# Layer B's weights of keys, values and output projection: high and low parts made by rounding and adding transfers in place of Vector's subtraction

## The chip, the cores and the metric

The kernel runs on one core of a Trainium2 chip. The metric is the device time of one execution in microseconds (us). The engines that matter are TensorE (PE, matmuls; PEld is its weight load), VectorE (DVE), ScalarE (ACT), GpSimd (POOL), and SyncE (SP), which here only issues transfers. Each engine works through its own instructions strictly in order. A transfer (DMA) is issued by SP, ACT or POOL and is then carried out by 16 DMA engines that all issuers share; whoever needs the data waits on a semaphore.

## The reference, cut to what matters

Two layers with 512 tokens and width 1024. The second layer, B, computes (leaving out what the change does not touch):

```
s_in = rmsnorm(h, ln_shared)
kvf  = s_in @ w_shared_kv            # keys 768 | values 768 | forget gate 12
q    = rmsnorm(h, ln_mix_pre) @ w_in_b
main = forgetting_attention(q, k, v, log_f)      # 12 heads of 64, blocks of 128 queries
mixed = concat([main, memory_attention(q_mem, mem_n, w_mem_kv)])
h = h + rmsnorm(mixed @ w_out, ln_mix_post)      # then the feed-forward part
```

All of it is float32. The matrices that the change touches are the key part and the value part of `w_shared_kv` and the `w_out` of layer B.

## The kernel before, in words

**Products of two parts.** TensorE is fed with a rounded float32 format (`F32R`). To keep accuracy each operand is held as a high part (the value rounded) and a low part (the value less its high part), and a product is three matmuls, high by high, low by high and high by low (`mm3`; L174 to L176 are its lines). So every weight has to be made into two parts before TensorE can use it. Before, that goes as follows: SP loads 128 x 1024 floats (512 KB) into a buffer `raw` (four of these exist, and every weight of the kernel goes through them); for each half of 512 columns ACT copies into `hi`, which rounds (L222), and Vector subtracts, `lo = raw - hi` (L223). `hi` and `lo` have eight half-size buffers each. As soon as the two splits are done, `raw` is free for the next load.

```
def split(src, hi, lo, eng=None):
    A.copy(hi, src)
    (eng or V).tensor_sub(lo, src, hi)
```

**Layer B.** Its work around the change runs in this order. The query weights go through four blocks of a `boundary` with the feed-forward part before, and four more (`ps` in the trace). Then the products of keys and values: three value blocks of two loads each, six key blocks of one load each. These are cut into pieces (a value piece is 12 matmuls, a key piece 6), and a list `fill` sets each block's loading three pieces before its first piece. Six pieces run at once; the others are strewn between the steps of the attention heads, four memory heads and twelve forgetting heads, to give TensorE something to do while a head's softmax (DVE and ACT) runs. During the heads' last part the pieces of the output projection's first half (`out_part`, blocks of columns dh 0 and dh 1 with two loads each, matmuls called `y<-whi,mixedhi` in the trace) take the place of the keys and values. What remains of the projection (`mix_tail`, four loads) runs after the heads, two of its four loads into other buffers ("aside").

**A head.** Per block of 128 queries: logits on TensorE (`lg`), the row maximum on DVE (L412), the exponential on ACT (L413), the normalisation on DVE (`p<-p,sm`, L422), transposes on TensorE (`tr`), their two parts by ACT and DVE (`pT`), and the product with the values (`o`, L497). ACT and DVE do these in line with the splitting of the weights.

**What sets the order.** The kernel is written against a framework that assigns each engine its sequence of instructions when the program is built, by its own estimate of when operands will be there. The order is fixed after that, and each engine waits at an instruction until its semaphores are met. POOL does very little before the change: a few power functions for the norms (L237) and four copies of 128 KB between halves of the memory keys (`memk`, L364). SP issues the weight loads and, for each pair of heads, transfers that lay out query and key parts (L1194 to L1196).

Of the kernel before, what the change touches and what calls it, by code (L numbers as in the profile page):

```python
# [8 lines left out]
F32R = mybir.dt.float32r  # L9
BF16 = mybir.dt.bfloat16  # L10
AF = mybir.ActivationFunctionType
ALU = mybir.AluOpType
# [3 lines left out]
P = 128  # L16
T = 512
D = 1024
KT = 8
# [21 lines left out]
def hybrid(ctx: ExitStack, tc: tile.TileContext, i: dict, out: bass.AP):  # L41
# [5 lines left out]
    wp = ctx.enter_context(tc.tile_pool(name="weights", bufs=4))  # L47
# [4 lines left out]
    last_load, last_exp = [None], [None]  # L52

    def name(s):
        n_of[s] = n_of.get(s, 0) + 1
        return f"{s}_{n_of[s]}"

    def act(s, dt=F32R, shape=(P, T)):
        return ap.tile(list(shape), dt, tag="a", name=name(s))

    def plain(s, shape=(P, T), dt=F32):
        return yp.tile(list(shape), dt, tag="y", name=name(s))
# [10 lines left out]
    def ps(tag, shape=(P, T), s="ps"):  # L73
        return pp.tile(list(shape), F32, tag=tag, name=name(s), bufs=2 if tag == "tr" else 3)

    V, A, PE, G = nc.vector, nc.scalar, nc.tensor, nc.gpsimd
# [37 lines left out]
    def pair_of_parts(n=512, aside=False):  # L114
        if aside:
            return act("whi"), act("wlo")
        return (wp.tile([P, 512], F32R, tag="hi", name=name("whi"), bufs=8)[:, :n],
                wp.tile([P, 512], F32R, tag="lo", name=name("wlo"), bufs=8)[:, :n])
# [11 lines left out]
    def prepared(src, shape, eng=None):  # L130

        raw = wp.tile([P, 1024], F32, tag="raw", name=name("raw"), bufs=4)
        n = shape[0] * shape[1]
        dst = raw[:, :n].rearrange("p (a b) -> p a b", a=src.shape[1]) if len(src.shape) == 3 else raw[:, :n]
        last_load[0] = nc.sync.dma_start(dst, src)
        return weight_parts(raw, shape, eng)

    def weight_parts(raw, shape, eng=None):
        n = shape[0] * shape[1]
        parts = []  # L140
        for d in range(0, n, 512):
            pair = pair_of_parts(min(512, n - d))
            split(raw[:, d : min(d + 512, n)], *pair, eng)
            parts += cut(pair, shape[1])
        return parts

    def moving_pair(src, aside=False):

        raw = wp.tile([P, 1024], F32, tag="raw", name=name("raw"), bufs=4)
        last_load[0] = nc.sync.dma_start(raw.rearrange("p (m c) -> p m c", m=4), src)  # L150
        four = raw.rearrange("p (m k c) -> p m k c", m=4, k=2)
        parts = []
        for x in range(2):
            hi, lo = (t.rearrange("p (m c) -> p m c", m=4) for t in pair_of_parts(aside=aside))
            split(four[:, :, x, :], hi, lo)
            parts.append((hi, lo))
        return parts

    def out_weights(layer, kp, dh, aside=False):
        return moving_pair(i["w_out"][layer, 4 * dh : 4 * dh + 4, :, 256 * kp : 256 * kp + 256]  # L160
                           .rearrange("m p c -> p m c"), aside)

    def down_weights(layer, k, dh, aside=False):
        return moving_pair(i["w_down"][layer, 4 * dh : 4 * dh + 4, :, k : k + 2, :]
                           .rearrange("m p k c -> p m (k c)"), aside)
# [6 lines left out]
    def mm3(o, w, x, start, stop, more=False):  # L172

        PE.matmul(o, w[0], x[0], start=start, stop=False, skip_group_check=more)  # L174
        PE.matmul(o, w[0], x[1], start=False, stop=False, skip_group_check=more)  # L175
        PE.matmul(o, w[1], x[0], start=False, stop=stop, skip_group_check=more)  # L176
# [44 lines left out]
# [3 lines that stand above are left out]
# [525 lines left out]
    def out_part(layer, mixed):  # L749


        ys = [[None] * 2 for _ in range(TB)]

        def block(dh):
            w, o = [], []

            def load():
                for kp in range(2):
                    w.extend(out_weights(layer, kp, dh))

            def piece(tb, n):
                if n == 0:
                    o.append(ps("mm", s="y"))
                for k in range(2 * n, 2 * n + 2):
                    token_products(o[tb], mixed[ORDER[k]], w[k], tb, k == 0, k == 3)
                if n == 1:
                    ys[tb][dh] = plain("y")
                    A.copy(ys[tb][dh], o[tb])

            return load, [lambda tb=tb, n=n: piece(tb, n) for tb in range(TB) for n in range(2)]  # L770

        return ys, [block(dh) for dh in range(2)]

    def mix_tail(layer, mixed, ys):
        return tail_of([mixed[k] for k in ORDER[4:]], lambda kp, dh, aside: out_weights(layer, 2 + kp, dh, aside), ys)
# [263 lines left out]
    def layer_b(phase, fp):  # L1039
# [34 lines left out]
        def key_block(m):  # L1074

            w, o = [], []

            def load():
                w.extend(prepared(i["w_k"][m], (KT, P)))

            def piece(n):
                if n == 0:
                    o.append(ps("mm", s="k"))
                for k in range(2 * n, 2 * n + 2):
                    mm3(o[0], w[k], s_act[k], k == 0, k == KT - 1)
                if n == 3:
                    keys.append(act("k", F32))
                    V.tensor_mul(keys[m], o[0], rbc)

            return load, [lambda n=n: piece(n) for n in range(4)]  # L1090

        def value_block(j):

            w, o = [], []

            def load():
                for kh in range(2):
                    w.extend(prepared(i["w_v"][j, kh], (4, 256)))

            def piece(tk, kh):  # L1100
                if kh == 0:
                    o.append(ps("mm", (P, 256), s="v"))
                c = slice(tk * P, (tk + 1) * P)
                for k in range(4 * kh, 4 * kh + 4):
                    mm3(o[tk], (s_act[k][0][:, c], s_act[k][1][:, c]), w[k], k == 0, k == KT - 1)
                if kh:
                    if tk % 2 == 0:
                        vals[j, tk // 2] = plain("vf", (P, 2, 256))
                    V.tensor_scalar_mul(vals[j, tk // 2][:, tk % 2, :], o[tk], r4b[:, tk : tk + 1])

            return load, [lambda tk=tk, kh=kh: piece(tk, kh) for tk in range(TB) for kh in range(2)]
# [11 lines left out]
        for k in range(KT):  # L1123
            w = wfs[:, k, :, :].rearrange("p a b -> p (a b)")
# [74 lines left out]
        for n in range(HEADS):  # L1199
            pr, j = divmod(n, 2)  # L1200
# [114 lines left out]
```

## Time and profile before

| | us |
|---|---|
| median of 3 runs | 1136.09 |
| lowest, highest | 1135.89, 1137.71 |
| the profiled execution's own time | 1135.76 |
| its span, first to last instruction | 1134.0 |
| PE busy in the span | 1112.0 (98%) |
| DVE busy | 897.7 (79%) |
| ACT busy | 657.4 (58%) |
| POOL busy | 24.1 (2%) |
| layer B's heads, in the span | about 604 to 745 |

How to read it: a row of work says start, duration, engine, line, operation, and output<-inputs with their shapes; where idle time came before it, a bracket at the end names what ended that idle time. PE's matmuls overlap in the pipeline, so one that shows 0.39 us may follow the one ahead by 0.23 us. Buffer numbers are left out in the trace's names; in the lists of order below they are kept.

### The profile page before, as it was taken

Reading aid. Unit: us, or ns where it says so; the run is one execution under the profiler, and the core shown is the slowest. Engines: PE = TensorE matmul, PEld = TensorE weight load, DVE = VectorE, ACT = ScalarE, POOL = GpSimd, SP = SyncE. Lnnn points to the kernel's source line nnn. Section 1 sums busy time; section 2 is a strip of 40 time slices with the busy share of each in tenths; the row PEclk is TensorE's granted clock in tenths of the full one; section 3 lists DMA queues with packets and bytes.
Section 4 is the critical chain, followed back from the end, with each engine's and each line's share of the span. In section 5 each row is a group of like instructions: output and inputs, shape, how many; then the busy total and the mean of one; then the engine's idle time right before and its main releaser. Section 6 shows DMA issues by size and latency. Waiting matters only on the chain.

```text
span 1134.0 us, 19608 instructions
## 1 busy us (share of the span) xinstructions
PE 1112.0 (98%) x7437; PEld 1018.8 (90%) x7437; DVE 897.7 (79%) x1727; ACT 657.4 (58%) x1367; POOL 24.1 (2%) x42
## 2 busy tenths in 40 slices
PE   7999999999999999999999999999999999999997
PEld 6998889999899898997978998889999899899995
DVE  7979558898698588786957889958998588588775
ACT  6665458665266254476737667858765266255453
POOL 1000000000000000001000000000000000000000
PEclk9999999999999999999999999999999999999999
DMA  8412231325234233243232455521134224233222
GB/s 280 133 45 93 92 95 57 114 93 156 67 112 131 61 107 112 78 148 129 78 110 73 115 125 136 137 90 43 62 120 149 75 83 141 75 106 118 75 75 75
DMA packets 63814, 118.13 MB, mean 104 GB/s; under 512 B 5164, under 2 KB 39992, under 8 KB 63720
## 3 DMA queue, kind: packets, MB, share of 16 engines
q1 hardware_dynamic: 63384, 116.31, 33.2%
q8 instruction: 58, 0.95, 0.3%
q0 software_dynamic: 192, 0.52, 0.2%
q14 instruction: 36, 0.29, 0.1%
q10 hardware_dynamic: 144, 0.05, 0.0%
HBM read 104.71 MB, written 2.10 MB: 94 GB/s over the span
## 4 chain that ended last, share of the span: by engine, by line
PE 83%; DVE 8%; ACT 4%; DMA 2%; issue 2%; POOL 0%; SPq 0%; POOLq 0%; DVEq 0%; ACTq 0%
PE y L176 8%; PE y L175 8%; PE y L174 8%; PE a L175 5%; PE a L174 5%; PE a L176 5%; PE ps L174 4%; PE ps L175 4%; PE ps L176 4%; PE e L174 3%; PE e L176 3%; PE e L175 3%; PE x L176 3%; PE x L175 3%; PE x L174 3%
## 5 line engine op out<-in xcount | busy, mean ns | idle before, releaser
L222 ACT CAST whi<-raw 128x512 fp32r<-128x512 f32 x460 | 276.6, 620 | 267.4 <-PE y L176 111.2
L223 DVE TENSOR_TENSOR wlo<-raw,whi 128x512 fp32r<-128x512 f32 x460 | 306.4, 686 | 114.6 <-ACT whi L222 110.3
L174 PE MATMUL y<-whi,fhi 128*128 128x512 f32 x352 | 137.7, 392 | 0.6 <-ACT whi L222 0.6
L175 PE MATMUL y<-wlo,fhi 128*128 128x512 f32 x352 | 137.2, 391 | 0.5 <-DVE wlo L223 0.5
L176 PE MATMUL y<-whi,flo 128*128 128x512 f32 x352 | 137.2, 390 | 0.1
L174 PE MATMUL x<-xshi,whi 128*128 128x256 f32 x320 | 90.6, 283 | 0.0
L175 PE MATMUL x<-xslo,whi 128*128 128x256 f32 x320 | 90.6, 283 | 0.0
L176 PE MATMUL x<-xshi,wlo 128*128 128x256 f32 x320 | 90.6, 283 | 0.0
L175 PE MATMUL a<-xslo,whi 128*128 128x256 f32 x320 | 90.5, 283 | 0.0
L174 PE MATMUL a<-xshi,whi 128*128 128x256 f32 x320 | 90.5, 283 | 0.0
L176 PE MATMUL a<-xshi,wlo 128*128 128x256 f32 x320 | 90.4, 283 | 0.0
L174 PEld LDWEIGHTS y<-whi,fhi 128*128 128x128 f32 x352 | 66.1, 188 | 15.4 <-ACT whi L222 1.5
L176 PEld LDWEIGHTS y<-whi,flo 128*128 128x128 f32 x352 | 66.1, 188 | 14.8 <-DVE flo L223 1.2
L175 PEld LDWEIGHTS y<-wlo,fhi 128*128 128x128 f32 x352 | 66.1, 188 | 14.7 <-DVE wlo L223 1.6
L174 PE MATMUL ps<-xshi,whi 128*128 128x256 f32 (+1 forms) x224 | 67.8, 305 | 0.0
L176 PE MATMUL ps<-xshi,wlo 128*128 128x256 f32 (+1 forms) x224 | 66.8, 300 | 0.0
L175 PE MATMUL ps<-xslo,whi 128*128 128x256 f32 (+1 forms) x224 | 66.2, 298 | 0.0
L174 PEld LDWEIGHTS a<-xshi,whi 128*128 128x128 f32 x320 | 61.4, 192 | 0.3
L175 PEld LDWEIGHTS a<-xslo,whi 128*128 128x128 f32 x320 | 61.4, 192 | 0.3
L174 PEld LDWEIGHTS x<-xshi,whi 128*128 128x128 f32 x320 | 61.4, 192 | 0.0
L175 PEld LDWEIGHTS x<-xslo,whi 128*128 128x128 f32 x320 | 61.4, 192 | 0.0
L176 PEld LDWEIGHTS x<-xshi,wlo 128*128 128x128 f32 x320 | 61.4, 192 | 0.0
(285 smaller groups left out, 3111.8 us busy)
## 6 DMA issues: line engine op xcount, KB each, us to landing
raw<-in_w_gate SPq DMA_DIRECT2D x44, 512.0 KB
raw<-in_w_up SPq DMA_DIRECT2D x44, 512.0 KB
raw<-in_w_down SPq DMA_DIRECT2D x44, 512.0 KB
raw<-in_w_out SPq DMA_DIRECT2D x16, 512.0 KB
raw<-in_w_b_q SPq DMA_DIRECT2D x8, 512.0 KB
raw<-in_w_a_v SPq DMA_DIRECT2D x6, 512.0 KB
raw<-in_w_a_u SPq DMA_DIRECT2D x6, 512.0 KB
raw<-in_w_v SPq DMA_DIRECT2D x6, 512.0 KB
```

The lines of the kernel that those rows point to most:

```text
L174: PE.matmul(o, w[0], x[0], start=start, stop=False, skip_group_check=more)
L175: PE.matmul(o, w[0], x[1], start=False, stop=False, skip_group_check=more)
L176: PE.matmul(o, w[1], x[0], start=False, stop=stop, skip_group_check=more)
L222: A.copy(hi, src)
L223: (eng or V).tensor_sub(lo, src, hi)
```

## The change

The 18 loads of layer B's key, value and output weights, except the two aside ones, are made in another way. GpSimd issues a transfer from memory into a tile of the rounded type, so that the transfer itself rounds: this is the high part, in a buffer of the group `raw`, and TensorE reads it from there. For each half ACT then writes the negated high part into a `lo` buffer, and GpSimd issues a second transfer of the same weights that adds to what lies there: `lo = -hi + weight`. Vector's subtraction is gone, ACT's copy has become ACT's negated copy, SP's 18 loads have become 18 rounding and 36 adding transfers on GpSimd's queue, and the weights are read from memory twice. A `raw` buffer is now free only when TensorE has done its last matmul with it, and the eight `hi` buffers are not used by these weights.

```
+    def fetched(src):
+        hi = wp.tile([P, 1024], F32R, tag="raw", name=name("whi"), bufs=4)
+        lo = [wp.tile([P, 512], F32R, tag="lo", name=name("wlo"), bufs=8) for _ in range(2)]
+        return hi, lo
+
+    def fetched_rows(src, shape):
+        hi, lo = fetched(src)
+        last_load[0] = G.dma_start(hi, src)
+        for x in range(2):
+            c = slice(512 * x, 512 * x + 512)
+            A.activation(lo[x], hi[:, c], AF.Copy, scale=-1.0)
+            G.dma_start(lo[x], src[:, c], accum_op=ALU.add)
+        w = shape[1]
+        return [(hi[:, d : d + w], lo[d // 512][:, d % 512 : d % 512 + w]) for d in range(0, 1024, w)]
+
+    def fetched_pair(src):
+        hi, lo = fetched(src)
+        hi = hi.rearrange("p (m c) -> p m c", m=4)
+        last_load[0] = G.dma_start(hi, src)
+        parts = []
+        for x in range(2):
+            c = slice(P * x, P * x + P)
+            part = lo[x].rearrange("p (m c) -> p m c", m=4)
+            A.activation(part, hi[:, :, c], AF.Copy, scale=-1.0)
+            G.dma_start(part, src[:, :, c], accum_op=ALU.add)
+            parts.append((hi[:, :, c], part))
+        return parts
+
-    def moving_pair(src, aside=False):
+    def moving_pair(src, aside=False, fetch=False):
+        if fetch:
+            return fetched_pair(src)
...
     def out_weights(layer, kp, dh, aside=False):
         return moving_pair(i["w_out"][layer, 4 * dh : 4 * dh + 4, :, 256 * kp : 256 * kp + 256]
-                           .rearrange("m p c -> p m c"), aside)
+                           .rearrange("m p c -> p m c"), aside, layer == 1 and not aside)
...
-                w.extend(prepared(i["w_k"][m], (KT, P)))
+                w.extend(fetched_rows(i["w_k"][m], (KT, P)))
...
-                    w.extend(prepared(i["w_v"][j, kh], (4, 256)))
+                    w.extend(fetched_rows(i["w_v"][j, kh], (4, 256)))
```

A key or value row is one run of 4 KB per partition (2 KB in an adding transfer): 128 runs. An output load takes four runs of 1 KB per partition (512 B in an adding transfer): 512 runs.

The order of TensorE's matmuls through the heads is the same before and after. On the other engines it moves, and the prediction speaks of two places.

The first is the queue that carries the output weights. Before, this is SP's queue, here at the load of the fourth output block; a load stands between the heads' transfers and waits only for a free `raw`:

```order
L1194 DMA qc_7072<-whi_8181 64x512
L1194 DMA kc_7074<-wlo_8184 64x512
L1195 DMA qc_7072<-cc 2x512
L1196 DMA kc_7074<-cc 2x512
L150 DMA raw_8797<-in_w_out 128x4x256
L1194 DMA qc_7071<-whi_8414 64x512
L1195 DMA qc_7071<-cc 2x512
```

After, it is POOL's queue. whi_8759 and whi_8767 are the high parts of the second column block (dh 1); wlo_8551 to wlo_8560 are the four low parts of the first block, wlo_8760 to wlo_8769 those of the second; whi_9021 and whi_9029 are the high parts of the tail's two loads, whose four low parts follow:

```order
L169 DMA whi_8759<-in_w_out 128x4x256
L175 DMA wlo_8551<-in_w_out 128x4x128
L175 DMA wlo_8552<-in_w_out 128x4x128
L175 DMA wlo_8559<-in_w_out 128x4x128
L175 DMA wlo_8560<-in_w_out 128x4x128
L169 DMA whi_8767<-in_w_out 128x4x256
L175 DMA wlo_8760<-in_w_out 128x4x128
L175 DMA wlo_8761<-in_w_out 128x4x128
L175 DMA wlo_8768<-in_w_out 128x4x128
L175 DMA wlo_8769<-in_w_out 128x4x128
L169 DMA whi_9021<-in_w_out 128x4x256
L169 DMA whi_9029<-in_w_out 128x4x256
```

The first block's low parts now stand behind whi_8759, which waits for the last high-part matmul of the fifth key block, whose buffer it takes; whi_9021 and whi_9029 wait for the first block's last matmuls, since they take its buffers.

The second place is ACT's row of the last head. Before, the four copies of the tail's first two weight loads (whi_9055 to whi_9069) stand ahead of that head's exponentials (p_8883 on):

```order
L222 CAST whi_9065<-raw_9063 128x512
L768 COPY y_8868<-y_8848 128x512
L222 CAST pT_8871<-tr_8870 128x512
L222 CAST mixedhi_8733<-f_8735 128x512
L222 CAST whi_9069<-raw_9063 128x512
L222 CAST pT_8887<-tr_8886 128x512
L413 ACTIVATE p_8883,sm_7110<-lg_8879,nmx_7109 128x512
L413 ACTIVATE p_8899,sm_7110<-lg_8895,nmx_7109 128x384
L222 CAST pT_8923<-tr_8922 128x256
L413 ACTIVATE p_8916,sm_7110<-lg_8912,nmx_7109 128x256
```

After, the four negated copies stand among the exponentials (wlo_9022 and wlo_9023 wait for whi_9021 to land, wlo_9030 for whi_9029):

```order
L447 ACTIVATE p_8851,sm_7104<-lg_8847,nmx_7103 128x512
L174 ACTIVATE wlo_9022<-whi_9021 128x512
L174 ACTIVATE wlo_9023<-whi_9021 128x512
L447 ACTIVATE p_8867,sm_7104<-lg_8863,nmx_7103 128x384
L174 ACTIVATE wlo_9030<-whi_9029 128x512
L447 ACTIVATE p_8884,sm_7104<-lg_8880,nmx_7103 128x256
L256 CAST pT_8891<-tr_8890 128x256
L174 ACTIVATE wlo_9031<-whi_9029 128x512
L802 COPY y_8903<-y_8870 128x512
L447 ACTIVATE p_8867,sm_7104<-lg_8905,nmx_7103 128x128
```

What moved there: three exponentials and a `pT` now stand behind instructions that wait for transfers. The third value block (high parts whi_7810 and whi_7818) has the same pattern among the exponentials of the second forgetting head: its first negated copy follows that head's first exponential.

## The prediction

> **What bounds the kernel now.** I read the page's first part, then the stretches of the heads, then PE's waits, and last the chain of waits where DVE is fullest.
>
> ```profile
> span 1134.0 us, 19608 instructions
> PE 1112.0 (98%) x7437; PEld 1018.8 (90%) x7437; DVE 897.7 (79%) x1727; ACT 657.4 (58%) x1367; POOL 24.1 (2%) x42
> L222 ACT CAST whi<-raw 128x512 fp32r<-128x512 f32 x460 | 276.6, 620 | 267.4 <-PE y L176 111.2
> L223 DVE TENSOR_TENSOR wlo<-raw,whi 128x512 fp32r<-128x512 f32 x460 | 306.4, 686 | 114.6 <-ACT whi L222 110.3
> ```
>
> PE is the bound: 22 us of the span are left over, 1134.0 less 1112.0. Work taken from DVE pays only where PE stands idle for DVE. The stretches of the heads and PE's waits from 570 to 762 us say where that is:
>
> ```profile
> core 0: us, PE busy (x) PEld busy (x) DVE busy (x) ACT busy (x) POOL busy (x), PEclk, DMA share, GB/s
> 680.00:720.00 40.00, 38.77 (x233) 33.49 (x232) 37.63 (x90) 29.89 (x78) 0.00 (x0) 1.00 0.62 145
> 720.00:760.00 40.00, 39.90 (x208) 33.68 (x207) 27.56 (x57) 27.74 (x63) 0.55 (x1) 1.00 0.37 114
> PE mlg L446 <- ACT mp L413: 1.0, 1, 1.0
> PE tr L429 <- DVE p L422: 0.6, 1, 0.6
> PE lg L476 <- ACT p L413: 0.4, 1, 0.4
> PE o L497 <- DVE pT L223: 0.2, 1, 0.2
> ```
>
> DVE is 94% busy from 680 to 720 us (37.63 of 40), and PE idles 1.23 us there. In the rest PE hardly waits. In that stretch the chain of waits runs through DVE, and these are the weights' subtractions on it:
>
> ```profile
> 697.98 0.67 DVE wlo L223
> 701.85 0.60 DVE wlo L223
> 703.91 0.59 DVE wlo L223
> 710.94 0.59 DVE wlo L223
> ```
>
> **What is removed.** 36 subtractions, at 686 ns 24.7 us of DVE. Nearly all lie beside a busy PE. What they are worth is between 0 (PE waits for something else next) and the 2.45 us of the four rows above; I take PE's visible idle time of that stretch, **-1.2 us**. ACT's 36 copies become 36 negated copies. The nearest row is ACT's other copy with a factor of -1, at the same length per partition, 0.63 us against 0.62: nothing.
>
> ```profile
> 604.05 0.63 ACT L1170 ACTIVATE cc<-cc 12x512 fp32r<-12x512 f32 x1
> ```
>
> SP loses 18 loads. Behind them on its queue stand the heads' transfers, and no wait of PE above names one of those: nothing. PE's matmuls and their order stay.
>
> **What is added: 54 transfers on POOL.** POOL has few rows of its own before; its only transfers are four of 128 KB between partitions, in 64 runs of 2 KB:
>
> ```profile
> L364 POOL DMA_DIRECT2D memk<-memk x4: 523/524/726, 510.9 to 512.6; - x4
> DMA to landing us min/median/max: 2.9/3.2/3.7
> 497.40 5.31 DMA raw<-in_w_mem_v
> 509.09 3.53 DMA raw<-in_w_b_q
> q1 hardware_dynamic: 63384, 116.31, 33.2%
> ```
>
> POOL is occupied 0.52 us for one, and 2.7 us later it has landed (3.2 less 0.52). The two rows from the chain are 512 KB loads issued by SP, 5.3 and 3.5 us. Neither a rounding nor an adding transfer is in this trace. I need three prices:
> - POOL's time for one transfer, g. If it is per transfer, 0.52. If it goes with the runs, 1.05 for the 128 runs of keys and values, and 4.2 for the 512 runs of the output weights (0.524 x 512 / 64). For keys and values I take 0.8, the middle. For the output weights I take 3, in the upper half: most of them have a third stream, the old value that is read.
> - From there to the landing of a rounding transfer: 2.7 to 5.3; I take 4, the middle.
> - The same of an adding transfer: 2.7 to 5.3 as far as rows go; I take 5.3, since it fetches two operands.
>
> The DMA engines themselves have room: 116.31 MB took 33.2% of the span, 3.24 us per MB, so the second reading of 9.4 MB takes 31 us, or 61 if adding counts double, of the 150 us in which 38 to 62% is free.
>
> **The third value block, +1.0.** Its buffers come free in time, but on POOL its high parts stand behind the low parts of the fourth key block, and those wait for ACT's negated copies, which wait for a `lo` buffer, whose last reader is the second block's last low part:
>
> ```profile
> 642.45 0.28 PE L175 MATMUL v<-wlo,shi 128*128 128x256 f32 x1
> 646.06 0.69 ACT L413 ACTIVATE p<-lg,nmx 128x512 f32<-128x512 f32 x1 [1.18 <-DVE nmx L412]
> 647.70 0.36 ACT L222 CAST pT<-tr 128x256 fp32r<-128x256 f32 x1
> 650.68 0.39 PE L497 MATMUL o<-pT,vals 128*128 128x256 f32 x2
> ```
>
> At 642.4 the first of the two low parts can be issued, so the three transfers end at 644.8 and whi_7810 lands at 648.8. ACT reaches the negated copy at 646.75 and waits 2.05 us. Behind it stand two exponentials and the `pT` of 647.70, which comes at 651.2; with DVE's half it is ready at 651.7 for a product that ran at 650.68. Ends: 0 with the lowest prices, 3.1 with the highest. PE waits for ACT there.
>
> **The output's first block, +2.6.** Its four low parts stand on POOL behind whi_8759, which waits for PE's last high-part matmul of the fifth key block:
>
> ```profile
> 694.35 0.39 PE L175 MATMUL k<-slo,whi 128*128 128x512 f32 x1
> 709.09 0.39 PE L175 MATMUL y<-wlo,mixedhi 128*128 128x512 f32 x1
> 712.32 0.40 PE L175 MATMUL y<-wlo,mixedhi 128*128 128x512 f32 x1
> ```
>
> From 694.6 five transfers of 3 us end at 709.6, and the fourth low part lands at 714.9, where PE wants it at 712.3 (the first lands at 705.9, wanted at 709.1): 2.6 late. Up to g = 2.5 there is no loss, beyond that 5 us for each us of g; at 4.2, 8.4.
>
> **The tail's loads and the last head, +4.4.** The two low parts ahead are issued when ACT gets to them, about 722.5. Then whi_9021 waits for the buffer whose last reader runs at 728.08, then whi_9029, then four low parts.
>
> ```profile
> 722.46 0.59 ACT L222 CAST pT<-tr 128x512 fp32r<-128x512 f32 x1 [0.92 <-PE tr L429]
> 728.08 0.40 PE L176 MATMUL y<-whi,mixedlo 128*128 128x512 f32 x1
> 734.03 0.69 ACT L413 ACTIVATE p<-lg,nmx 128x512 f32<-128x512 f32 x1 [0.47 <-DVE nmx L412]
> 737.84 0.40 PE L497 MATMUL o<-pT,vals 128*128 128x256 f32 x2
> 739.47 1.03 PE L429 MATMUL tr<-ident,p 128*128 128x128 f32 x8
> 747.58 0.39 PE L175 MATMUL y<-wlo,mixedhi 128*128 128x512 f32 x1
> 749.62 0.39 PE L175 MATMUL y<-wlo,mixedhi 128*128 128x512 f32 x1
> ```
>
> The two end at 729.1, whi_9021 at 732.1 (landed 736.1), whi_9029 at 735.1 (739.1). ACT ends its exponential at 734.7 and waits for each; the `pT` behind the second wait is done at 740.6, with DVE's half 741.0, for the product of 737.84: 3.2 late; the transposes of 739.47 that want all the exponentials are 3.3 late. The low parts then end at 739.7 to 748.7 and the last lands at 754.0, wanted at 749.6 plus the 3.3: 1.1 more. With the lowest prices nothing, with the highest 8.7 and 4.8. In this stretch PE is 39.90 of 40 busy, so nothing swallows it.
>
> **High parts in `raw`.** Buffers are held until PE is done, so the two aside loads wait for the second block's last matmuls and then have some 4.5 us; the loss is 0 to 1.3 and lies inside the tail's delay: not added.
>
> **The sum.** 1.0 + 2.6 + 4.4 - 1.2 = 6.8 us on the profiled execution's 1135.76, that is 1142.6; the median of the runs stands 0.33 higher: **1142.9**. All lowest prices with the largest gain give 1136.1 - 2.5 = 1133.6; all highest 1136.1 + 3.1 + 8.4 + 13.5 = 1161.
>
> [...] The memory-key row gives 3.2 us for 128 KB. [...]
>
> **The rivals.** I count a change as one from 0.2% (2.3 us), about what a measurement of this kernel can tell.
> - *No difference* (chance 0.13): POOL's time per transfer is under 2 us, so all weights land in time, and ACT's moved copies cost what DVE's relief gives: 1.0 + 0.8 - 1.2, near 1136.7. For it speaks that the weights have 15 to 20 us from a free buffer to their use; against it, that they share one queue.
> - *Faster* (0.19): POOL's price is 0.52 for every transfer, the landings 2.7, ACT waits for nothing, and the four subtractions come off the chain: 1136.1 - 2.5 = 1133.6. It decides at g below about 1 for the output weights and needs PE's hidden stalls at 690 to 715 to be DVE's; the 94% speaks for it, the 1.23 us of idle time against it.
> [...]
> - *Dear transfers* (0.15): POOL's time goes with the runs, or adding is slower than any row: 1153 to 1161 or beyond; speaks for it that nothing in the trace bounds an adding transfer from above.
> - *Weights late by several us* (the forecast, 0.43): 1139 to 1151.
>
> That the transfer might not round would change the low parts, not a duration.
>
> So slower holds 0.43 + 0.10 + 0.15 = 0.68, the same 0.13, faster 0.19. The range runs from 1134, into the faster case, to 1159, into the dear one, and leaves out some 0.08 below and 0.10 above.
>
> **What would show it.** Right: POOL rows of some 3 us for the output weights; PE waiting for DMA `wlo<-in_w_out` near 712, for `pT` or `p` of ACT near 650 and 738, and ACT idle for DMA `whi<-in_w_out` near 735; DVE under 34 of 40 at 680 to 720. Wrong: POOL rows near 0.5 us and landings under 4 us, or PE waits elsewhere, at the first value block or in the feed-forward part behind it.

## The result and the profile after

The changed kernel took 1154.96 us (median of 4 runs, 1152.48 to 1157.53) against 1135.99 us before: a ratio of 1.0166, 95% interval 1.0149 to 1.0182, or 18.9 us. 1142.9 had been forecast; the sign was right, the size was not. The profiled execution took 1152.48 us, 2.5 below the median, with a span of 1150.7; all that follows compares this span with the 1134.0 of before. All lines of the kernel stand 34 further down from here on.

The page of the kernel after: span, busy time of the engines, the groups of the copies and subtractions, and the DMA queues (packets, MB, share of 16 engines).

```profile
span 1150.7 us, 19646 instructions
PE 1119.2 (97%) x7437; PEld 1022.8 (89%) x7437; DVE 880.9 (77%) x1691; ACT 656.6 (57%) x1367; POOL 72.1 (6%) x96
L256 ACT CAST whi<-raw 128x512 fp32r<-128x512 f32 x424 | 256.0, 620 | 259.7 <-PE y L210 110.5
L257 DVE TENSOR_TENSOR wlo<-raw,whi 128x512 fp32r<-128x512 f32 x424 | 282.9, 688 | 108.5 <-ACT whi L256 106.8
q1 hardware_dynamic: 58488, 106.87, 31.1%
q0 software_dynamic: 14880, 19.40, 9.1%
```

The 36 casts and 36 subtractions are gone as forecast. But PE, with the same 7437 matmuls, is busy 7.2 us longer (1119.2 against 1112.0) and idle 9.5 us longer (31.5 against 22.0). Together these are the 16.7 us of the span.

Where they lie is seen in the stretches of the heads. First three of before, then four of after (columns as in the prediction: PE busy, PEld, DVE, ACT, POOL, granted clock, DMA share, GB/s).

```profile
640.00:660.00 20.00, 20.00 (x124) 17.83 (x124) 17.99 (x40) 14.54 (x35) 0.00 (x0) 1.00 0.62 165
700.00:720.00 20.00, 18.77 (x110) 16.00 (x110) 19.62 (x48) 14.83 (x42) 0.00 (x0) 1.00 0.79 182
720.00:740.00 20.00, 20.00 (x117) 17.42 (x116) 16.51 (x39) 15.55 (x39) 0.00 (x0) 1.00 0.41 121
```

```profile
640.00:660.00 20.00, 16.56 (x88) 14.16 (x88) 10.02 (x25) 9.96 (x24) 7.13 (x9) 0.84 0.97 198
660.00:680.00 20.00, 19.43 (x132) 17.88 (x131) 14.91 (x36) 12.19 (x33) 2.25 (x3) 0.99 0.77 172
700.00:720.00 20.00, 19.45 (x115) 16.39 (x113) 17.41 (x42) 15.07 (x40) 7.70 (x7) 1.00 0.98 167
720.00:740.00 20.00, 14.68 (x70) 12.56 (x70) 10.30 (x24) 10.65 (x26) 3.79 (x4) 0.83 0.75 135
```

Two stretches carry nearly all: 640 to 660 and 720 to 740 us. In both PE stands idle and its granted clock is low (0.84 and 0.83 in the mean); the DMA share is 0.97 in the first and 0.98 just ahead of the second. Following the same matmul through both traces gives the same picture: its start is 0.4 us later than before from 630 to 650 us, 6.9 us at 654, 7.5 at 710, 15.3 at 717, 16.2 at 754 and 17.1 from 790 on (times of the kernel before). The first stall costs 6.5 us, the second 7.8; the rest comes in steps of 1 us and less.

The order of the matmuls isn't quite the same, as had been stated. By the traces 107 of the 7437 stand at another place, most of them behind the heads, the others at 610 to 620 and at 713 to 715 us. At the last of these, eight transposes (`tr`) stood behind six logits matmuls before; now four of them stand ahead of the six, and four amid them.

The waits of PE and of ACT between 600 and 780 us, kernel after, that belong to the two stalls (total, times, longest):

```profile
PE tr L463 <- DVE p L456: 4.7, 2, 4.2
PE o L531 <- ACT pT L256: 3.4, 1, 3.4
PE y L209 <- DMA wlo<-in_w_out: 1.2, 1, 1.2
ACT wlo L160 <- DMA whi<-in_w_v: 5.7, 1, 5.7
ACT wlo L174 <- DMA qa<-wlo: 4.8, 1, 4.8
```

**The first stall.** The timeline of the kernel after, POOL, ACT, PE:

```profile
642.29 1.73 POOL L161 DMA_DIRECT2D wlo<-in_w_k  x2 [16.08 <-ACT wlo L160]
643.39 1.75 POOL L157 DMA_DIRECT2D whi<-in_w_v  x2
645.72 0.69 ACT L447 ACTIVATE p<-lg,nmx 128x512 f32<-128x512 f32 x1 [0.39 <-DVE nmx L446]
652.18 0.63 ACT L160 ACTIVATE wlo<-whi 128x512 fp32r<-128x512 f32 x1 [5.68 <-DMA whi<-in_w_v]
654.66 1.04 PE L531 MATMUL o<-pT,vals 128*128 128x256 f32 x2 [3.44 <-ACT pT L256]
655.92 0.63 PE L209 MATMUL k<-slo,whi 128*128 128x512 f32 x1
```

POOL has waited 16 us for ACT's copies of the fourth key block; then it issues two adding and two rounding transfers, 1.5 MB, within 3 us. ACT reaches the negated copy of the third value block after its exponential of 645.72 and stands 5.68 us, until the rounding transfer has landed; the exponentials and the `pT` behind it are late, and PE idles 3.44 us. That is the place and the mechanism of the prediction's "third value block". The last row is new: the matmul after the stall takes 0.63 us where the same form took 0.39. By slices of 2 us the granted clock is 0.91, 0.50, 0.50, 0.50 and 0.88 from 652 to 662 us, and 1.00 again after.

**The second stall.** The same kernel, POOL, SP, ACT and PE from 707 to 727 us:

```profile
707.15 0.59 SPq L1228 DMA_DIRECT2D qa<-wlo  x1
707.30 5.26 POOL L175 DMA_DIRECT2D wlo<-in_w_out  x4 [3.64 <-DVE pT L257]
715.37 1.73 SPq L1228 DMA_DIRECT2D qa<-wlo  x1
718.15 0.63 ACT L174 ACTIVATE wlo<-whi 128x512 fp32r<-128x512 f32 x1
723.62 0.63 ACT L174 ACTIVATE wlo<-whi 128x512 fp32r<-128x512 f32 x1 [4.84 <-DMA qa<-wlo]
721.18 0.50 PE L209 MATMUL y<-wlo,mixedhi 128*128 128x512 f32 x1 [1.16 <-DMA wlo<-in_w_out]
726.06 1.09 PE L463 MATMUL tr<-ident,p 128*128 128x128 f32 x4 [4.15 <-DVE p L456]
```

Four adding transfers of the output's first block go out from 707.3 to 712.6 us. While these (and a rounding one of 713.67) are under way, the head's own transfers, SP's, crawl: the one of 715.37 occupies SP 1.73 us where the same transfer of the head before, at 707.15, took 0.59, and ACT's wait for it ends at 723.6. ACT's second copy writes a `lo` tile out of the ring that this transfer still reads, so ACT stands 4.84 us, with an exponential and a head's `vals` behind it. PE first misses a low part (1.16 us) and then the normalised probabilities (4.15 us), and again works at half clock: 0.50 in each slice from 726 to 732 us. The other order of the matmuls can be only a small part of this: the six logits matmuls that could have run ahead of the transposes take 1.2 us before, and they read the query that came at 723.6.

Last, POOL's transfers from 560 to 760 us, in groups (busy, mean ns):

```profile
L175 POOL DMA_DIRECT2D wlo<-in_w_out x12 | 15.6, 1548 | 27.5 <-DVE f L432 11.3 <-ACT wlo L174 7.6 <-DVE vals L257 4.7
L161 POOL DMA_DIRECT2D wlo<-in_w_v x12 | 10.6, 909 | 18.3 <-ACT wlo L160 18.2
L169 POOL DMA_DIRECT2D whi<-in_w_out x6 | 5.2, 870 | 17.1 <-PE k L210 11.9 <-PE o L531 3.7 <-PE y L210 0.9
L157 POOL DMA_DIRECT2D whi<-in_w_k x6 | 3.6, 605 | 10.0 <-DVE wlo L257 4.6 <-PE k L210 3.6 <-PE k L209 1.7
```

POOL itself is quick: 0.6 to 1.5 us for a transfer in the mean, and busy 47 us of the 190 from 570 to 760. The landings, counted from the issue, are not: 3.8 to 10.9 us for a rounding transfer, 3.7 to 11.1 us for an adding one.

### The profile page after: what moved, and what is told of

It is laid out like the page before. It is cut to its first block, busy times and chain, and to the rows that moved or that the text cites. A ratio compares the mean times of both kernels' runs of the same rounds, so it can differ in the third digit from the quotient of the medians.

```text
span 1150.7 us, 19646 instructions
## 1 busy us (share of the span) xinstructions
PE 1119.2 (97%) x7437; PEld 1022.8 (89%) x7437; DVE 880.9 (77%) x1691; ACT 656.6 (57%) x1367; POOL 72.1 (6%) x96
## 4 chain that ended last, share of the span: by engine, by line
PE 77%; issue 6%; DVE 6%; ACT 4%; DMA 4%; POOL 2%; SPq 1%; POOLq 0%; DVEq 0%; ACTq 0%
PE y L210 8%; PE y L209 8%; PE y L208 8%; PE a L210 5%; PE a L209 5%; PE a L208 5%; PE ps L208 4%; PE ps L209 4%; PE ps L210 4%; PE e L208 3%; PE e L210 3%; PE e L209 3%; PE x L210 3%; PE x L209 3%; PE x L208 3%
## 5 line engine op out<-in xcount | busy, mean ns | idle before, releaser
L256 ACT CAST whi<-raw 128x512 fp32r<-128x512 f32 x424 | 256.0, 620 | 259.7 <-PE y L210 110.5
L257 DVE TENSOR_TENSOR wlo<-raw,whi 128x512 fp32r<-128x512 f32 x424 | 282.9, 688 | 108.5 <-ACT whi L256 106.8
```

## The experiments

All times are against runs of the kernel before on the same chip. "+x us" is the ratio less one, times 1136.

**Keys and values alone.** `out_weights` back to the loads of before.

```diff
-  .rearrange("m p c -> p m c"), aside, layer == 1 and not aside)
+  .rearrange("m p c -> p m c"), aside)
```

> Keys and values come by rounding and adding transfers as in the changed kernel; the output weights of layer B are loaded and subtracted as before. First theory (two separate stalls: ACT stands in its queue for a landing among the exponentials at 646 and again at 719 us, PE runs dry for 3.4 and 5.3 us, and each time its clock falls for some microseconds after): the first stall stays whole, the second is gone, so 6.5 to 8 us over the kernel before, near 1143.5. Rival (POOL's one queue and the DMA engines are overfull through all the heads, and the loss grows with the bytes): 12 of 18 weights, so two thirds of the 19 us, near 1148.5, with delays after 690 us too.

Measured: 1146.47 us, ratio 1.0082 (1.0065 to 1.0099), +9.3 us. The five runs lie far apart, 1143.8 to 1152.7, and the profiled one is the slowest: there the first stall is 4.39 us long (ACT waits 6.6 us for `whi<-in_w_v`), and two more of 2.2 and 1.9 us, which the changed kernel doesn't have, stand at 626 and 684 us.

```profile
PE o L531 <- ACT pT L256: 4.4, 1, 4.4
ACT wlo L160 <- DMA whi<-in_w_v: 6.6, 1, 6.6
```

The time lies between the two theories' (1143.5 and 1148.5) and doesn't choose. The trace does: the first stall is there, and from 700 us on nothing is added. About half of the loss is in the keys and values.

**Output weights alone.** `key_block` and `value_block` call `prepared` again.

> Only the six output weights come by rounding and adding transfers; keys and values are loaded and subtracted as before. First theory (two separate stalls): no delay before 700 us, then the second stall with 7 to 8 us and the tail's 1 to 2, near 1145. Rival (the second stall comes of the shift that the first one makes, and of the keys' transfers still under way): under 3 us, near 1138. Second rival (loss by bytes): a third of 19 us, near 1142, spread over the stretch.

Measured: 1142.23 us, 1.0054 (1.0033 to 1.0075), +6.1 us. In the profile (span 1142.5) the second stall is there without the first: PE waits 1.3 and 1.9 us at 715 to 718 us, and the clock is 0.50 at 720 us.

```profile
ACT wlo L174 <- DMA qa<-wlo: 3.2, 1, 3.2
```

The time is the one that the loss by bytes would give (1142), but that was to be spread; the matmuls' delay grows by nearly 5 of this run's 8 us between 710 and 717 us. So the second stall doesn't come of the first; it is smaller than in the changed kernel.

**The negated copies on POOL.**

```diff
-            A.activation(lo[x], hi[:, c], AF.Copy, scale=-1.0)
+            G.tensor_scalar(out=lo[x], in0=hi[:, c], scalar1=-1.0, scalar2=None, op0=ALU.mult)
...   # the same for the output weights
```

> The 36 negated copies run on POOL, not on ACT; nothing else is changed. First theory (the stalls are ACT's queue, the weights themselves come in time): ACT no longer waits for landings, PE's waits of 3.4 and 4.2 us for pT and p go, and the clock stays full; what stays is a few microseconds where POOL, which now waits in order, brings output weights late: 1137 to 1143. Rival (the weights are late, or POOL's copies and DVE's instructions hold each other up): PE waits for DMA wlo instead, or DVE's times grow, 1150 or more.

Measured: 1149.09 us, 1.0116 (1.0101 to 1.0131), +13.2 us. The stretch of the first stall, and PE's longest wait:

```profile
640.00:660.00 20.00, 20.00 (x125) 17.88 (x124) 15.34 (x36) 11.25 (x31) 14.63 (x13) 1.00 0.89 187
PE lg L510 <- DMA qa<-wlo: 3.0, 1, 3.0
```

With ACT out of it the first stall is gone: PE is busy all 20 us at full clock, though the block's rounding transfers landed hardly sooner (at 651.1 and 654.5 us, against 652.2 and 654.5). So the first stall is ACT's queue, not a late weight. The second stays in another form: now PE waits for the query transfer itself. The forecast of 1137 to 1143 was missed by this, and by some 5 us lost in steps between 675 and 708 us, whose cause stays open; a POOL copy of 512 columns took 1.7 and 2.0 us in the mean of its two forms where ACT's takes 0.63.

**Plain transfers in place of adding ones.**

```diff
-            G.dma_start(lo[x], src[:, c], accum_op=ALU.add)
+            G.dma_start(lo[x], src[:, c])
...   # the same for the output weights
```

> The 36 adding transfers become plain ones of the same bytes and shape: the add is left out, so the low parts hold rounded weights. If the landings of 10 us (against 4 to 5 elsewhere) come of the adding, which makes the DMA engines do more per byte: landings near 4 to 5 us, ACT waits 2 us or less at both places, near 1139. If they come of the number of transfers and bytes alone: waits and time as in the changed kernel, 1152 to 1157.

Measured: 1147.63 us, 1.0098 (1.0073 to 1.0123), +11.1 us: 7.8 us of the 18.9 are the adding. ACT's waits from 560 to 790 us:

```profile
ACT wlo L160 <- DMA whi<-in_w_v: 6.2, 1, 6.2
ACT wlo L174 <- DMA qa<-wlo: 0.9, 1, 0.9
```

The two stalls part here. The wait for the query transfer falls from 4.8 to 0.9 us, and the PE gap of 4.15 us at the second place to 1.25, with full clock. The first stays whole (6.2 us on ACT, 3.94 on PE). Adding makes the second stall; the first has another cause.

It isn't the fullness of the DMA engines as such: without the add and without the second stall their share from 700 to 720 us (the packets' times summed, so it can pass 1) is higher than the changed kernel's 0.98.

```profile
700.00:720.00 20.00, 19.22 (x113) 16.46 (x111) 17.05 (x39) 15.09 (x39) 4.46 (x6) 1.00 1.13 182
```

What goes with the add is the slow issue of SP's transfers. Of the heads' 72 of 128 KB, ten occupy SP for over 0.9 us in the changed kernel, none in this run (at most 0.83), and one in the kernel before (1.47 us at 711.2).

**ACT's delay without any transfer, in pieces.** In the kernel before, one cast of the third value block's weights is made nine times more.

```diff
             pair = pair_of_parts(min(512, n - d))
+            for _ in range(again if d == 0 else 0):
+                A.copy(pair[0], raw[:, d : min(d + 512, n)])
```

> The kernel before, with ACT's first copy of the third value block repeated nine more times (9 x 0.62 = 5.6 us) among the exponentials, where the changed kernel's ACT waits 5.7 us for a landing. No transfer is added. If ACT's standing still is by itself enough for the first stall: PE idles some 3.4 us there for pT, its granted clock falls for some microseconds after, and the loss is 6 to 7 us, near 1142.5. If the clock falls only for another reason (transfers, writes): 3 to 4 us, near 1139.5. If the stall needs late weights: under 1 us.

Measured: 1137.38 us, 1.0006 (0.9997 to 1.0016). The nine copies were spread by the scheduler that orders the program between the exponentials from 642 to 652 us and filled ACT's gaps. This shows that 5 us more of work on ACT, spread out, cost at most 2 us there (1.0016); it doesn't answer what was asked.

**The same in one piece.** Eleven copies, each held behind the one before in ACT's order, and the next exponentials and casts behind the last.

```diff
+                with tc.issue_after(last_exp[0].ins):
+                    last_exp[0] = A.copy(pair[0], raw[:, d : min(d + 512, n)])
```

> The kernel before, with one of ACT's copies of the third value block repeated eleven times in one piece (11 x 0.52 = 5.7 us) ahead of a head's last exponential, in an order that lets nothing else of ACT slip in between. No transfer is added, no weight comes late. If PE's falling clock follows from its idling alone: PE idles 2 to 4.5 us, its granted clock then stands near 0.5 for 3 to 7 us, and the loss is 4 to 8 us, 1140 to 1144. If the clock fell because of the transfers: the idle time alone, at most 4 us, at full clock. If ACT's slack swallows it: under 1.5 us.

Measured: 1148.77 us, 1.0108 (1.0092 to 1.0123), +12.3 us, more than any theory said: the scheduler put a head's copy and four other casts into the block as well, so ACT was held from 657.2 to 666.9 us, and the order of the matmuls behind it changed, so the whole loss isn't the stall's. What the run was for is in two rows of its stretches and in PE's wait:

```profile
660.00:664.00 4.00, 2.54 (x14) 2.01 (x12) 1.84 (x3) 3.85 (x7) 0.00 (x0) 1.00 0.00 0
664.00:668.00 4.00, 1.97 (x7) 1.68 (x8) 2.14 (x4) 3.94 (x10) 0.00 (x0) 0.57 0.00 0
PE v L178 <- ACT whi L228: 3.3, 1, 3.3
```

PE waits 3.3 us, and its clock falls to 0.57 in a stretch in which no DMA engine moves a byte and POOL does nothing. So here the falling clock goes with PE's idling alone, without the transfers.

**The negated copies later in ACT's order.** `finish`, with the copies and adding transfers, runs two pieces after the rounding transfer was issued, each copy held behind the last exponential.

```diff
-            A.activation(lo[x], hi[:, c], AF.Copy, scale=-1.0)
-            G.dma_start(lo[x], src[:, c], accum_op=ALU.add)
+        def finish():
+            for x in range(2):
+                c = slice(512 * x, 512 * x + 512)
+                after_exp(lambda: A.activation(lo[x], hi[:, c], AF.Copy, scale=-1.0))
+                G.dma_start(lo[x], src[:, c], accum_op=ALU.add)
+        ends.append(finish)
```

> The changed kernel with the negated copies placed two pieces of a block later in ACT's order, so that ACT reaches them after the rounding transfers have landed; the transfers themselves, their sizes and queue stay. If the loss is ACT's standing in its queue among the exponentials: both waits under 1 us and 1138 to 1144. If the low parts now come late, PE waits for DMA wlo instead: 1146 or more.

Measured: 1181.62 us, 1.0401 (1.0385 to 1.0416), +45.6 us. ACT waits for no landing of these weights any more; PE does:

```profile
PE k L232 <- DMA wlo<-in_w_k: 9.9, 4, 4.2
PE v L231 <- DMA wlo<-in_w_v: 6.6, 5, 2.2
PE y L231 <- DMA wlo<-in_w_out: 6.5, 5, 2.5
```

The rival's case, in full. These waits are 23 us; the span grew by 45.3, of which PE's busy time, the same matmuls, by 20.3 (1132.3). With the copies two pieces later the adding transfers go out too late for their use; what ACT is spared, PE waits.

**Twice as many buffers for the high parts.** Every second load puts them into the ring of high parts.

```diff
+        turn[0] += 1
+        if turn[0] % 2:
+            hi = [wp.tile([P, 1024], F32R, tag="raw", name=name("whi"), bufs=4)]
+        else:
+            hi = [wp.tile([P, 512], F32R, tag="hi", name=name("whi"), bufs=8) for _ in range(2)]
```

> The changed kernel, but every second load puts its high parts into two 512-column tiles of the ring of high parts (two rounding transfers of 256 KB) instead of one tile of the raw ring, so about twice as many loads can be under way. If the rounding transfer of the third value block lands late because its buffer comes free late: it is issued several microseconds earlier, ACT's wait there falls from 5.7 to under 1 us, the first stall goes and the second stays, 1145 to 1149. If it lands late because the DMA engines are overfull: no change, 1152 to 1157.

Measured: 1146.23 us, 1.0084 (1.0069 to 1.0099), +9.5 us: half of the loss is won. ACT's wait of 5.7 us for the third value block's rounding transfers is gone: they go out from 604.4 to 633.1 us and have landed by 636.2, instead of going out at 643.4 and 643.9.

Two things changed at once there. In the changed kernel the buffer is held until PE's last matmul on the block before, which ends at 643.3 us. And POOL had the low parts of the fourth key block ahead, which it could issue only from 642.3 on; in this run's order these stand behind the value block's rounding transfers. In the changed kernel the two conditions end together, and no run here separates them. At the same place ACT now waits for the next thing:

```profile
ACT wlo L172 <- DMA kc<-wlo: 5.1, 1, 5.1
ACT wlo L193 <- DMA qa<-wlo: 2.7, 1, 2.7
```

That is a `lo` tile which a head's transfer still reads, the second stall's mechanism. PE's gaps are 2.3 and 3.3 us, and the clock falls to 0.50 for 3.4 us after each.

**Longer runs.** The adding transfers of the output weights take two row blocks with all columns (256 runs of 1 KB) instead of four with half (512 of 512 bytes); the values land in the wrong places.

```diff
-            G.dma_start(part, src[:, :, c], accum_op=ALU.add)
+            G.dma_start(lo[x].rearrange("p (m c) -> p m c", m=2), src[:, 2 * x : 2 * x + 2, :], accum_op=ALU.add)
```

> The changed kernel, but each adding transfer of the output weights takes two row blocks with all 256 columns (256 runs of 1 KB) instead of four with 128 (512 runs of 512 bytes); the bytes are the same, the values land in the wrong places. If the second stall comes of the short runs of the adding transfers: their landing falls towards the keys' 4.7 us, the wait for the query transfer shrinks, and 4 to 7 us are won, 1148 to 1151. If it is the adding or the bytes as such: no change, 1152 to 1157.

Measured: 1151.76 us, 1.0134 (1.0117 to 1.0151). Some 3.7 us below the changed kernel, with intervals that just touch; ACT's wait for the query transfer is 4.2 us instead of 4.8. By the medians the length of the runs is a small part.

**The rings exchanged.** High parts in two tiles of the ring of high parts, low parts in one 1024-column tile of `raw` by one adding transfer.

```diff
+        hi = [wp.tile([P, 512], F32R, tag="hi", name=name("whi"), bufs=8) for _ in range(2)]
+        lo = wp.tile([P, 1024], F32R, tag="raw", name=name("wlo"), bufs=4)
```

> The changed kernel with the two rings exchanged: a load's high parts go into two 512-column tiles of the ring of high parts (two rounding transfers), its low parts into one 1024-column tile of the raw ring, made by one adding transfer of 512 KB instead of two of 256 KB, with runs twice as long. A low part no longer waits for a head's transfer out of the ring of low parts. If the stalls are ACT's waits for such buffers and for late rounding loads: both ACT waits under 2 us and 1138 to 1143. If the DMA engines' work as such decides: 1147 or more.

Measured: 1162.8 us, 1.022 (1.0204 to 1.0236), +25.0 us, against the expectation. ACT's waits:

```profile
ACT wlo L161 <- DMA whi<-in_w_k: 21.5, 9, 7.4
ACT wlo L161 <- DMA whi<-in_w_v: 21.0, 6, 8.8
```

The ring of high parts is shared with the heads' own parts. The third value block's first rounding transfer starts at 645.9 us instead of 643.4, and ACT stops 18 times for a rounding transfer, three of them of the output weights. A wait for a `lo` tile was exchanged for a dearer one. Half as many adding transfers didn't make up for it.

**Only the two last key blocks.**

```diff
-                w.extend(prepared(i["w_k"][m], (KT, P)))
+                w.extend((fetched_rows if m > 3 else prepared)(i["w_k"][m], (KT, P)))
...   # values and output weights as in the kernel before
```

> Only the fourth and fifth key blocks' weights (of blocks 0 to 5) come by rounding and adding transfers, four subtractions less for DVE just where it is busiest (690 to 715 us); all other weights as before. If DVE's relief is worth PE's idle time there: 1 us faster, 1135. If PE's short waits there are not DVE's subtractions: within 0.5 us of before. If two fetched blocks already stall ACT: 1138 or more.

Measured: 1135.90 us (11 runs), 0.9998 (0.9990 to 1.0007), -1.1 to +0.8 us: no stall, and no gain that can be told from nothing. But the run doesn't test what it was meant to. The four subtractions that it removes stood at 659.2, 662.5, 680.6 and 684.5 us, ahead of the stretch where DVE was fullest, and DVE there is hardly freer (37.63 of 40 before):

```profile
680.00:720.00 40.00, 38.66 (x233) 33.29 (x232) 37.02 (x89) 29.59 (x77) 1.72 (x2) 1.00 0.69 165
```

**Both causes at once.** Two rings and plain transfers.

> Both at once: every second load's high parts in the ring of high parts, and plain transfers in place of the adding ones (the add is left out, the low parts hold rounded weights). Alone the rings won 8.7 us and the missing add 7.3 us of the changed kernel's 19. If they are two causes of two stalls (rounding loads late for want of a buffer at 646 us, head transfers late beside the adding at 719 us), they add up: 1139, with no wait of PE over 1.5 us from 600 to 760 us and a full clock. If both act on the same stalls: 1143 or more.

Measured: 1141.40 us, 1.0047 (1.0031 to 1.0062), +5.3 us. PE's longest wait from 560 to 830 us is the one that before has too:

```profile
PE mlg L499 <- ACT mp L466: 1.0, 1, 1.0
PE o L550 <- ACT pT L275: 0.9, 1, 0.9
```

ACT's waits for a `lo` tile don't all go (3.7 us for `qa<-wlo`, 2.2 us for `kc<-wlo`), but PE stands at most 0.9 us for them. The clock is full through all the heads. The two changes account for 13.6 of the 18.9 us. They don't quite add up (7.8 + 9.4 would be 17.2): the rings alone had already taken 3.7 us from the second stall (4.1 instead of 7.8), which the plain transfers take away too. Of the 4.6 us that this span is longer, 3.1 are PE's busy time at full clock, spread over many small delays; what they are stays open.

This is also the kernel in which DVE's relief can be read, since nothing stalls at 712 us: from 690 to 715 us (times of the kernel before) the matmuls' delay shrinks from 3.6 to 2.8 us. So the relief is worth at most some 0.8 us here (the order of a few matmuls differs too), less than what the change costs elsewhere, and no kernel here beats the one before.

## Why the prediction was right and wrong

Slower was right. Of the 16.7 us by which the span grew, 14.3 lie where two steps of the prediction failed. The third value block, sized at 1.0 us, took 6.5. And the effect on the heads' own transfers, put at nothing since "no wait of PE above names one of those" and "the DMA engines themselves have room", made most of the second stall of 7.8. The time lies inside the range that was given, but the range was built from other losses, so this is luck.

| step | forecast | measured |
|---|---|---|
| DVE relief, 680 to 720 us | -1.2 | -0.45 by 708 us, then hidden by the second stall; at most some -0.8 in the kernel without stalls |
| third value block | +1.0 | +6.5 |
| output's first block | +2.6 | 1.2, inside the second stall |
| ACT waiting for a `lo` tile, second output block | not seen | most of +7.8 |
| tail's loads and last head | +4.4 | +0.9 up to 754 us, +0.9 behind |

*The relief.* PE's visible idle time was nearer than the 2.45 us of the rows on the chain: at most some 0.8 of its 1.2 us came. That DVE was 94% busy and stood on the chain didn't mean that PE waited for each subtraction.

*The third value block.* The mechanism was right down to the instruction: ACT waits among the exponentials, PE for `pT`. Two sizes were off. The landing of the rounding transfer was taken as 4 us from the end of its issue; here 1.5 MB were issued within 3 us beside a head's transfers, and it took 7.6. That made ACT's wait 5.7 us instead of 2.05. And the forecast counted idle time alone: the 3.4 us of idle time were followed by about 3 us lost to the clock.

*The output's first block.* POOL's time was taken as 3 us each, in the upper half; it was 1.3 (5.26 us for four). It goes only weakly with the runs: adding, 0.85 us for 128 and 1.3 us for 512 in the median. The fourth low part still came late, 1.2 instead of 2.6 us, for two reasons that the term hadn't. POOL stood 3.64 us before the first of them, until ACT had made the negated copies (the first ended at 707.0 us); and the fourth landed 8.6 us after its issue ended, not 5.3. The price was put on POOL's occupation when it lay in the copy and the landing.

*What was not seen.* The forecast followed each new transfer to its own user. It did not follow what the new transfers do to the heads' transfers beside them: the `qa<-wlo` that came late was there before and is untouched by the diff. "The DMA engines themselves have room" was said of 150 us as a whole; in the stretches that decide, the share rose from 0.62 to 0.97 and from 0.79 to 0.98. In sum the queue of POOL took 9.1% of 1150.7, 105 us of all 16 engines for 19.4 MB, 5.4 us per MB, against 3.35 for SP's queue; by the prediction's prices both readings together would have taken 61 us, or 92 with adding counted double. The adding is 11 us of it (8.2% of 1148.0 with plain transfers). Why an adding transfer holds up SP's issue stays open.

*The tail and the last head.* ACT waited 1.2 us for `whi<-in_w_out` and PE for nothing long. With POOL at 0.8 to 1.3 us for a transfer this term goes to its lower end, as its bounds said.

*The clock.* Of the 16.7 us, 7.2 are PE's own longer busy time. The row was in the trace of before: at its very end, from 1128 us on, PE idles and the granted clock is 0.65 and then 0.50. The forecast had no term for it. In the changed kernel the clock stood at 0.50 for 6.8 us at each of the two stalls (the slices of 652 to 662 us above add up to that), and in other runs for 3.4 us, as with the output weights alone. By estimate such a stretch costs up to half of its length beyond the gap, 3.4 or 1.7 us; at the first stall it was about 3 (6.5 less 3.44). The length of the gap ahead was measured too: in the heads of all these runs every gap of PE from 2.1 us on had the clock fall, of those between 1.6 and 2.0 us four did and one did not (1.9 us at 710 us, with the negated copies on POOL), and none up to 1.4 us did that stood alone.

*The rivals.* "Dear transfers" (0.15) names the time that came, 1153 to 1161, and half of its reason: adding was dear, though not by POOL's time. The 0.10 in the sum of the chances is for POOL and DVE getting in each other's way. No run shows that a transfer of POOL's has to wait for DVE: they took 0.6 to 1.5 us in the mean of their groups. DVE's normalisation of 512 columns took 506 ns in the mean against 478 before, and with the negated copies on POOL 530 (for 256 columns 529 against 353); what lengthened it is not shown. That POOL's price is per transfer, 0.52 us by the row of the memory keys, nearly held for rounding transfers (0.56 us in the median for keys and values), less for adding ones (0.85 and 1.32). It didn't make the change cheap, since the landings were not small (3.7 to 11.1 us).

## What to carry to other kernels

A copy that waits for a transfer is dear among the instructions that PE is waiting for next: what it costs is not the weight's lateness but all that is queued behind it (here 5.68 us of ACT's waiting, and 3.44 us of PE's behind it). (Placing it later is no cure if the next transfer waits for it; here that was dearer, +45.6 us.) When transfers are added, follow also what they do to the transfers that were there before: how long those take (one of SP's here 1.73 us to issue instead of 0.59), and which buffers they still hold. A mean over the kernel doesn't show it, and here the share of busy DMA engines didn't either. And when PE may run dry for some 2 us or more, count up to 1.7 or 3.4 us on top of the gap, an estimate: half of the 3.4 or 6.8 us for which its clock fell here.

## What was unexpected of the hardware

- After a gap of 1.6 us and more in PE's work in the heads the granted clock stood at 0.50 for 3.4 or 6.8 us, once for 13.7 with further gaps in it (the copies later in ACT's order, 742 to 755 us); one gap of 1.9 us is an exception (copies on POOL, 710 us). It did so without any transfer under way too (0.57 in the mean from 664 to 668 us, DMA share 0.00, the copies in one piece); gaps up to 1.4 us that stood alone left it at 1.00.
- POOL was occupied 0.56 us (median) by a rounding transfer of 128 runs and 0.77 us by one of 512, but 0.85 and 1.32 us by adding ones of half the bytes; the same transfers without the add took 0.54 and 0.74 us.
- A rounding transfer of 512 KB landed in 3.8 us at best and 10.9 us at worst, in the changed kernel; loads of one form differ as much (`whi<-in_w_v` 3.8 to 10.6), so it isn't the form.
- SP's issue of a head's 128 KB transfer, 0.59 us in the median, took up to 1.73 us beside adding transfers and at most 0.83 beside plain ones, though the DMA share was higher with these (1.13 against 0.98 at 700 to 720 us).
